# norm_g on the transposed rows: the first token group of a hybrid encoder layer, prepared two chunks at a time

## Chip, core and metric

The kernel runs on one core of one Trainium2 chip. The metric is device time in microseconds (us) of one execution. TensorE is called PE here, VectorE DVE, ScalarE ACT, GpSimd POOL, SyncE SP.

## What is computed

One encoder layer over two inputs, 1024 and 512 tokens of 1024 channels, in fp32. Cut to what matters here:

```python
h = rmsnorm(x, norm_g[l])          # x * rsqrt(mean(x*x) + EPS) * g
p = h @ w_in[l]                    # 1024 -> 4096 columns for three token mixers
y_a = conv_branch(...)             # glu(a_val, a_glu) -> depthwise conv of width 31 -> ...
y_b = sgu_branch(...)
y_c = hgrn_branch(...)
x = x + jnp.concatenate([y_a, y_b, y_c], axis=-1) @ w_out[l]
return rmsnorm(x, final_norm_g)
```

## The kernel before

Tokens stand in three groups of 512, each in four chunks of 128 rows. A matrix product in fp32 precision is made of three products in the fast format fp32r: both operands are split into a high part (a copy rounded to fp32r) and a low part (what the copy lost), and high x high, high x low and low x high are summed. `project` (L195) makes one 128-column tile of `h @ w_in` for one group, or for a half of it (`part`, 256 tokens), with 8 steps of three matmuls, L205 (weights high, tokens high), L206 (weights high, tokens low) and L207 (weights low, tokens high).

`prep` (L283) makes the tokens ready, and this is what the change rewrites for group 0. For each chunk `(g, c)`:

- `squares` (L289): ACT squares the 1024 channels of each row and sums them into `st`.
- `scaled` (L299): POOL makes the reciprocal root in two small operations (`rstd`, L118 and L119); DVE multiplies the rows by it and by `gb`, norm_g broadcast to all 128 partitions (L303). For odd chunks of groups 1 and 2, POOL multiplies by `gb` (`gained`, L295), and DVE by the root alone (L301).
- `turned` (L306): PE transposes the chunk in 8 blocks into two PSUM banks (L313); for each bank ACT writes the high part `hh` (128x512, L316) and DVE the low part `hl` (L317). Once a chunk is turned, `ready[g]` allows products.

`w_split` (L182) splits one weight tile `wr` into `wh` (ACT, L123) and `wl` (POOL, L124) in two halves and issues further weight loads. `warm` (L213) issues matmuls whose result is not used.

The order on ACT, DVE and POOL is the program's order (`manual_schedule`, L440); PE and SP are ordered by the scheduler when the program is built. Tasks such as `prep` are generators: `project` calls `step` every second of its 8 steps when it makes a half group, and `step` resumes a task whose time has come. Before the first product, `prep` prepares chunks 0 and 1 of group 0 and the squares and scaling of chunks 2 and 3; then the transposes of chunks 2 and 3; then, every `PACE` steps, one chunk of groups 1 and 2 (`rest`). The products of the two first column tiles (`pglu`, `pval`) are made for each half of each group.

SP issues the loads in the order x chunk 0, 1, `gb`, two halves of the first weight tile, x chunks 2, 3, the second weight tile, and the chunks of group 1 (L419 to L428).

Of the kernel before, what the change touches and what calls it, by code (L numbers as in the profile page):

```python
# [11 lines left out]
F32 = mybir.dt.float32  # L12
F32R = mybir.dt.float32r
# [7 lines left out]
P = 128  # L21
# [8 lines left out]
PJ = 3  # L30
NGAP = 2
PACE = 3
WARM = (18, 2, 0)
LOW = 32

FIRST = (2, 8, 32)
# [18 lines left out]
def trunk_kernel(ctx, tc, x_prompt, x_sample, norm_g, w_in, conv_w, conv_b, conv_ln_g, conv_ln_b,  # L55
# [25 lines left out]
    def tp_t(name):  # L81
        return ps_tp.tile([P, GRP], F32, tag="tp", name=name)

    def sc_t(name):
        return ps_sc.tile([P, NCH, P], F32, tag="sc", name=name)
# [32 lines left out]
            pool_e.tensor_scalar(out=out, in0=in_, scalar1=mul, scalar2=EPS, op0=ALU.mult, op1=ALU.add)  # L118
        pool_e.tensor_tensor(out=out, in0=out, in1=mexp[:, :n], op=ALU.pow)  # L119

    def split(hi, lo, src):

        act(hi, src, AF.Copy)  # L123
        pool_e.tensor_tensor(out=lo, in0=src, in1=hi.bitcast(F32), op=ALU.subtract)  # L124


# [52 lines left out]
                nc.sync.dma_start(raw, w_src[:, (n % 2) * 4:(n % 2) * 4 + 4, m * P:(m + 1) * P])  # L179
            w_raw.append(raw)  # L180

    def w_split():  # L182
        n = len(w_ready)
        if n < len(tile_order):
            hi = wp.tile([P, KT, P], F32R, tag="hi", name=f"wh{n}")
            lo = wp.tile([P, KT, P], F32R, tag="lo", name=f"wl{n}")
            for a in range(2):
                split(hi[:, 4 * a:4 * a + 4, :], lo[:, 4 * a:4 * a + 4, :], w_raw[2 * n + a])
                w_load()
            w_ready.append((hi, lo))  # L190

    hts = [None] * NG
    ready = [0] * NG

    def project(m, g, name, done, pj=None, part=slice(0, GRP)):  # L195

        hi, lo = w_ready[tile_order.index(m)]
        wait_for(lambda: ready[g] * P >= part.stop)
        his, los = hts[g]
        if pj is None:  # L200
            pj = pj_t(name)
        short = part.stop - part.start < GRP
        for k in range(KT):
            hh, hl = his[k // 4][:, k % 4, part], los[k // 4][:, k % 4, part]
            nc.tensor.matmul(pj[:, part], hi[:, k, :], hh, start=k == 0, stop=False)  # L205
            nc.tensor.matmul(pj[:, part], hi[:, k, :], hl, start=False, stop=False)  # L206
            nc.tensor.matmul(pj[:, part], lo[:, k, :], hh, start=False, stop=k == KT - 1)  # L207
            if k == KT - 1 and part.stop == GRP:
                done(pj)
            if not short or k % 2 == 1:  # L210
                step()

    def warm(n):  # L213

        t = uo_t("warm").rearrange("p c n -> p (c n)")
        for _ in range(n):
            nc.tensor.matmul(t[:, :P], ident, ident, start=True, stop=True)
# [62 lines left out]
        nc.sync.dma_start(xt, xsrc[g][c * P:(c + 1) * P, :])  # L280
        return xt

    def prep(xs, junk_t, gb):  # L283
# [21 lines left out]
        def turned(g, c):  # L305
# [11 lines left out]
                dve.tensor_tensor(out=lo, in0=tp3, in1=hi.bitcast(F32), op=ALU.subtract)  # L317
            ready[g] = c + 1

        warm(WARM[0])  # L320
        squares(0, 0)
        scaled(0, 0)
        squares(0, 1)
        scaled(0, 1)
        w_split()
        turned(0, 0)
        warm(WARM[1])
        turned(0, 1)
        warm(WARM[2])
        squares(0, 2)  # L330
        scaled(0, 2)
        squares(0, 3)
        scaled(0, 3)
        w_split()
        yield 4
        turned(0, 2)
        yield 2
        turned(0, 3)
        yield 1
        rest = [(g, c) for g in range(1, NG) for c in range(NCH)]  # L340
        for i in range(len(rest) + 2):
# [41 lines left out]
    def local_main(l1, accs):  # L383
# [11 lines left out]
        def glu_pair(i, g, parts=(slice(0, GRP),)):  # L395
            sg = sg_t(f"sglu{i}{g}")

            def val_done(pj):
                si, j = where(g)
                dve.tensor_tensor(out=glus[i][si][:, PAD + j * GRP:PAD + (j + 1) * GRP], in0=pj, in1=sg, op=ALU.mult)  # L400

            pg, pv = pj_t(f"pglu{i}{g}"), pj_t(f"pval{i}{g}")
            for part in parts:
                last = g == NG - 1 and part.stop == GRP
                project(A_GLU + i, g, "", lambda pj: act(sg, pj, AF.Sigmoid), pg, part)
                if last:
                    w_split()
                project(A_VAL + i, g, "", val_done, pv, part)
                if last:
                    w_split()  # L410

        with tc.tile_pool(name="xp", bufs=1) as xp:
            def x_t(shape, name):
                return xp.tile(shape, F32, tag="x", name=name, bufs=9)
# [4 lines left out]
            xs = [[] for _ in range(NG)]  # L419
            xs[0].append(load_x(0, 0, x_t))  # L420
            xs[0].append(load_x(0, 1, x_t))
            nc.sync.dma_start(gb, norm_g.broadcast_to((P, DM)))
            w_load()
            w_load()
            for c in range(2, NCH):
                xs[0].append(load_x(0, c, x_t))
            w_load(x_t([P, KT, P], "wr2"))
            xs[1] = [load_x(1, c, x_t) for c in range(NCH)]  # L428
            rows = xp.tile([N_ROWS, P], F32, tag="rows", name="rows")
            for r0, src in ((R_NG, norm_g[0]), (R_CB, conv_b[0]), (R_CLG, conv_ln_g[0]), (R_CLB, conv_ln_b[0]),  # L430
# [8 lines left out]
                    pool_e.memset(glus[i][si][:, PAD + len(gs) * GRP:], 0.0)  # L439
            with tc.manual_schedule(engines={mybir.EngineType.Activation, mybir.EngineType.DVE,  # L440
                                             mybir.EngineType.Pool}):
                task = prep(xs, junk_t, gb)
# [734 lines left out]
```

## Time and profile before

| what | value |
|---|---|
| device time, median of 3 runs | 850.74 us (849.82 to 851.8) |
| device time of the profiled execution | 850.33 us |
| its span, first to last instruction | 848.2 us |
| busy, share of the span: PE / DVE / ACT / POOL | 97% / 58% / 41% / 33% |
| mean granted clock of PE | 0.992 |

The span is 2.1 us shorter than the time of its execution. PE is busy nearly always, but the busy time of an engine is an average over stages; in the first 45 us several engines take turns in setting the pace. The mean granted clock is a share of 2.4 GHz.

### The profile page before, as it was taken

The page shows a single profiled execution, that of the slowest core. Times are in us where ns is not written, and L with a number is a line of the kernel's source. Part 1 is how long each engine was busy: PE and PEld are TensorE (multiplying, and loading weights), DVE is VectorE, ACT ScalarE, POOL GpSimd, SP SyncE. Part 2 cuts the span into 40 slices and gives each one's busy share as a digit, 9 for nine tenths or more (in the row PEclk, how much of TensorE's full clock was granted, in tenths as well). Part 3 has the DMA queues.
Part 4 walks back from the last instruction along what each step waited for, and adds up shares of the span by engine and source line. Part 5 has one row for each costly group of instructions (what it writes and reads, how often), then busy time and mean ns, then how long its engine had stood idle before and what let it go on. Part 6 is the DMA issues. An engine that isn't in the chain of part 4 may idle for free.

```text
span 848.2 us, 17598 instructions
## 1 busy us (share of the span) xinstructions
PE 821.6 (97%) x7249; PEld 704.0 (83%) x7249; DVE 488.5 (58%) x1024; ACT 349.2 (41%) x707; POOL 277.6 (33%) x288
## 2 busy tenths in 40 slices
PE   6999969999999999999999999999999999999996
PEld 6998869877888889998877888899888787888886
DVE  4737767686423378742279855886324888443332
ACT  5725456654334454432244533545123454222221
POOL 5737867999523321031112104211112010111111
PEclk9999979999999999999999999999999999999999
DMA  8305534441112100021010102001111484334421
GB/s 273 139 11 159 160 113 135 138 138 50 49 36 64 51 27 27 3 63 50 16 36 27 39 1 75 27 3 27 40 48 51 200 290 147 123 135 145 145 99 50
DMA packets 63842, 72.35 MB, mean 85 GB/s; under 512 B 3643, under 2 KB 46994, under 8 KB 62738
## 3 DMA queue, kind: packets, MB, share of 16 engines
q1 hardware_dynamic: 63762, 71.23, 25.5%
q8 instruction: 57, 0.93, 0.5%
q14 instruction: 23, 0.19, 0.1%
HBM read 50.25 MB, written 20.97 MB: 84 GB/s over the span
## 4 chain that ended last, share of the span: by engine, by line
PE 81%; DVE 6%; DMA 4%; issue 3%; ACT 3%; POOL 3%; SPq 1%; POOLq 0%; ACTq 0%; DVEq 0%
PE po L1061 5%; PE po L1063 5%; PE po L1062 5%; PE pf L205 5%; PE pf L207 5%; PE pf L206 5%; PE o L975 3%; PE pg L205 2%; DMA wor<-in_w_out_dram 2%; PE pq L205 2%; PE sc L808 2%; PE pg L206 2%; PE pg L207 2%; DVE Q L783 2%; PE pq L206 2%
## 5 line engine op out<-in xcount | busy, mean ns | idle before, releaser
L124 POOL TENSOR_TENSOR wl<-wr,wh 128x512 fp32r<-128x512 f32 x64 | 85.1, 1341 | 161.1 <-ACT wh L123 156.3
L476 DVE SCALAR_TENSOR_TENSOR ca<-glu,par,ca 128x512 f32<-128x512 f32 x120 | 80.6, 747 | 0.0
L1061 PE MATMUL po<-woh,yh 128*128 128x512 f32 (+1 forms) x200 | 77.4, 387 | 0.0
L205 PE MATMUL pf<-hh,wh 128*128 128x512 f32 x192 | 76.8, 400 | 0.0
L1062 PE MATMUL po<-wol,yh 128*128 128x512 f32 (+1 forms) x200 | 76.2, 381 | 0.0
L1063 PE MATMUL po<-woh,yl 128*128 128x512 f32 (+1 forms) x200 | 76.1, 381 | 0.0
L207 PE MATMUL pf<-hh,wl 128*128 128x512 f32 x192 | 75.0, 391 | 0.0
L206 PE MATMUL pf<-hl,wh 128*128 128x512 f32 x192 | 74.8, 390 | 0.0
L789 ACT ACTIVATE kc<-K 128x512 f32<-128x512 f32 x84 | 56.3, 674 | 40.3 <-DVE K L783 36.7
L501 POOL TENSOR_TENSOR part<-part,pr 128x512 f32<-128x512 f32 x54 | 68.5, 1285 | 3.8 <-ACT pr L500 3.8
L783 DVE TENSOR_TENSOR Q<-Q,T 128x256 f32<-128x256 f32 x144 | 65.4, 495 | 2.9 <-ACT q L819 2.0
L123 ACT ACTIVATE wh<-wr 128x512 fp32r<-128x512 f32 x64 | 39.0, 627 | 50.8 <-PE pf L206 20.6
L783 DVE TENSOR_TENSOR K<-K,T 128x256 f32<-128x256 f32 x144 | 54.9, 422 | 5.8
L727 DVE TENSOR_SCALAR Q<-Q,oml,lbt 128x512 f32<-128x512 f32 x24 | 17.8, 742 | 64.7 <-ACT Q L724 64.7
L1067 DVE TENSOR_TENSOR yx<-po,yx 128x512 f32<-128x512 f32 (+1 forms) x25 | 16.7, 669 | 56.1 <-PE po L1063 56.1
L780 POOL TENSOR_TENSOR ks<-K 128x512 f32<-128x512 f32 x12 | 16.4, 1365 | 99.6 <-ACT kc L789 53.7
L1063 PEld LDWEIGHTS po<-woh,yl 128*128 128x128 f32 x200 | 37.6, 188 | 7.5 <-DVE yl L1042 0.2
L1062 PEld LDWEIGHTS po<-wol,yh 128*128 128x128 f32 x200 | 37.7, 188 | 6.9
L1061 PEld LDWEIGHTS po<-woh,yh 128*128 128x128 f32 x200 | 37.6, 188 | 6.8
L207 PEld LDWEIGHTS pf<-hh,wl 128*128 128x128 f32 x192 | 36.0, 188 | 7.8
L1079 POOL TENSOR_TENSOR stf<-stf 128x1 f32<-128x1 f32 x12 | 4.1, 340 | 117.2 <-ACT yx L1068 117.2
L205 PEld LDWEIGHTS pf<-hh,wh 128*128 128x128 f32 x192 | 36.1, 188 | 7.0
(366 smaller groups left out, 2278.2 us busy)
## 6 DMA issues: line engine op xcount, KB each, us to landing
wr<-in_w_in_dram SPq DMA_DIRECT2D x62, 256.0 KB
out_dram<-yx SPq DMA_DIRECT2D x24, 256.0 KB
yx<-yd SPq DMA_DIRECT2D x12, 448.0 KB
x<-in_x_prompt_dram SPq DMA_DIRECT2D x8, 512.0 KB
wor<-in_w_out_dram SPq DMA_DIRECT2D x16, 256.0 KB
wod<-woh SPq DMA_DIRECT2D x16, 256.0 KB
wod<-wol SPq DMA_DIRECT2D x16, 256.0 KB
woh<-wod SPq DMA_DIRECT2D x4, 1024.0 KB
```

The costliest lines, as they stand in the source:

```text
L123: act(hi, src, AF.Copy)
L124: pool_e.tensor_tensor(out=lo, in0=src, in1=hi.bitcast(F32), op=ALU.subtract)
L205: nc.tensor.matmul(pj[:, part], hi[:, k, :], hh, start=k == 0, stop=False)
L206: nc.tensor.matmul(pj[:, part], hi[:, k, :], hl, start=False, stop=False)
L207: nc.tensor.matmul(pj[:, part], lo[:, k, :], hh, start=False, stop=k == KT - 1)
L476: dve.scalar_tensor_tensor(out=acc, in0=src, scalar=col(R_CW + 2 * t + i), in1=acc, op0=ALU.mult, op1=ALU.add)
L501: pool_e.tensor_tensor(out=parts[g], in0=parts[g], in1=pr, op=ALU.add)
L783: dve.tensor_tensor(out=x, in0=x, in1=y, op=ALU.mult)
L789: act(view(kc, 0, [[2 * m, n2], [m, 2], [1, m]]), view(K, 0, [[2 * m, n2], [GRP + m, 2], [1, m]]), AF.Copy)
L1061: nc.tensor.matmul(po, yh[:, k, :], hi[:, ns], start=k == 0, stop=False)
L1062: nc.tensor.matmul(po, yh[:, k, :], lo[:, ns], start=False, stop=False)
L1063: nc.tensor.matmul(po, yl[:, k, :], hi[:, ns], start=False, stop=k == KT - 1)
```

## The change

For group 0 alone, the rows are multiplied by the reciprocal root only (`scaled_first`, L353). norm_g is loaded as 8 rows of 128, issued from ACT's own queue, turned by PE into `gcol`, one column per block of 128 channels, and applied while the transposed rows leave PSUM: ACT writes the high part with `scale=gcol[:, k]`, DVE the low part as `src * gcol[:, k] - hi` (`gained_first`, L335). This is done for two chunks (256 tokens) at a time, and so per block of channels: a PSUM bank holds two blocks of 256 tokens. The broadcast `gb` is still loaded for groups 1 and 2, now behind the loads of group 0. The second weight tile is loaded before x chunks 2 and 3, and split inside `gained_first` with DVE in ACT's place. The first `pglu` and `pval` of group 0 put their eight matmuls with low weights last. The warm-up matmuls are 6 and 8 in place of 18 and 2.

```diff
-WARM = (18, 2, 0)
+WARM = (6, 8)
...
-    def split(hi, lo, src):
+    def split(hi, lo, src, by_vector=False):
 
-        act(hi, src, AF.Copy)
+        if by_vector:
+            dve.tensor_copy(hi, src)
+        else:
+            act(hi, src, AF.Copy)
         pool_e.tensor_tensor(out=lo, in0=src, in1=hi.bitcast(F32), op=ALU.subtract)
...
-            nc.tensor.matmul(pj[:, part], lo[:, k, :], hh, start=False, stop=k == KT - 1)
+            if not low_last:
+                nc.tensor.matmul(pj[:, part], lo[:, k, :], hh, start=False, stop=k == KT - 1)
+            elif k == KT - 1:
+                for j in range(KT):
+                    nc.tensor.matmul(pj[:, part], lo[:, j, :], his[j // 4][:, j % 4, part],
+                                     start=False, stop=j == KT - 1)
...
+        def turned_first(c0, tiles):
+            for c in (c0, c0 + 1):
+                for k in range(KT):
+                    o = (k % 2) * 256 + (c - c0) * P
+                    nc.tensor.transpose(tiles[k // 2][:, o:o + P], xs[0][c][:, k * P:(k + 1) * P], ident)
+                yield 1
+
+        def gained_first(c0, tiles, between=None):
+            his, los = hts[0]
+            ts = slice(c0 * P, (c0 + 2) * P)
+            for k in range(KT):
+                src = tiles[k // 2][:, (k % 2) * 256:(k % 2 + 1) * 256]
+                hi, lo = his[k // 4][:, k % 4, ts], los[k // 4][:, k % 4, ts]
+                act(hi, src, AF.Copy, scale=gcol[:, k:k + 1])
+                dve.scalar_tensor_tensor(out=lo, in0=src, scalar=gcol[:, k:k + 1], in1=hi.bitcast(F32),
+                                         op0=ALU.mult, op1=ALU.subtract)
+                if k == 5 and between:
+                    between()
+            ready[0] = c0 + 2
...
         warm(WARM[0])
-        squares(0, 0)
-        scaled(0, 0)
-        squares(0, 1)
-        scaled(0, 1)
+        gp = uo_t("gp").rearrange("p c n -> p (c n)")
+        nc.tensor.transpose(gp[:, :KT], gr, ident[:KT, :KT])
+        dve.tensor_copy(gcol, gp[:, :KT])
+        warm(WARM[1])
+        hts[0] = [[big.tile([P, 4, GRP], F32R, tag="H", name=f"h{e}0{a}") for a in range(2)] for e in "hl"]
+        for c in range(2):
+            squares(0, c)
+            scaled_first(c)
         w_split()
-        turned(0, 0)
...
-        turned(0, 1)
...
-        squares(0, 2)
-        scaled(0, 2)
-        squares(0, 3)
-        scaled(0, 3)
-        w_split()
-        yield 4
-        turned(0, 2)
-        yield 2
-        turned(0, 3)
+        tiles = four("txa")
+        for _ in turned_first(0, tiles):
+            pass
+        gained_first(0, tiles, lambda: w_split(True))
+        for c in range(2, NCH):
+            squares(0, c)
+            scaled_first(c)
+        yield 6
+        tiles = four("txb")
+        yield from turned_first(2, tiles)
+        gained_first(2, tiles)
         yield 1
...
-            nc.sync.dma_start(gb, norm_g.broadcast_to((P, DM)))
+            gr = xp.tile([KT, P], F32, tag="gr", name="gr")
+            gcol = xp.tile([P, KT], F32, tag="gcol", name="gcol")
+            nc.scalar.dma_start(gr, norm_g[0].rearrange("(r j) -> r j", j=P))
             w_load()
             w_load()
+            w_load(x_t([P, KT, P], "wr2"))
             for c in range(2, NCH):
                 xs[0].append(load_x(0, c, x_t))
-            w_load(x_t([P, KT, P], "wr2"))
+            nc.sync.dma_start(gb, norm_g.broadcast_to((P, DM)))
```

`yield 6` is the value that the first `next(task)` returns; it isn't used, as `yield 4` wasn't.

How the change moves instructions, at three places. First ACT, from the high parts of group 0's first half to the squares of group 1's first chunk. `hh` is the high part of the tokens, `tx`, `txa` and `txb` are PSUM tiles with transposed rows, `jx,st` the squares. Before:

```order
6 L316 ACTIVATE hh_194<-tx_198 128x4x128 [waits PE_49]
7 L316 ACTIVATE hh_195<-tx_205 128x4x128 [waits PE_49]
8 L316 ACTIVATE hh_194<-tx_215 128x4x128 [waits PE_49]
9 L316 ACTIVATE hh_195<-tx_222 128x4x128 [waits PE_49]
10 L289 ACTIVATE jx_231,st_230<-x_119 128x1024 [waits DMAHW5_49,Activation_49]
11 L289 ACTIVATE jx_237,st_236<-x_121 128x1024 [waits DMAHW6_49,Activation_49]
```

Now, for the second half of group 0 (the first half has the same eight rows with `txa`):

```order
17 L342 ACTIVATE hh_175<-txb_274,gcol 128x256 [waits PE_49]
18 L342 ACTIVATE hh_175<-txb_274,gcol 128x256 [waits DVE_49]
19 L342 ACTIVATE hh_175<-txb_275,gcol 128x256 [waits PE_49]
20 L342 ACTIVATE hh_175<-txb_275,gcol 128x256 [waits DVE_49]
21 L342 ACTIVATE hh_176<-txb_276,gcol 128x256 [waits PE_49]
22 L342 ACTIVATE hh_176<-txb_276,gcol 128x256 [waits DVE_49]
23 L342 ACTIVATE hh_176<-txb_277,gcol 128x256 [waits PE_49]
24 L342 ACTIVATE hh_176<-txb_277,gcol 128x256 [waits DVE_49]
25 L297 ACTIVATE jx_331,st_330<-x_128 128x1024 [waits DMAHW1_49,Activation_49,Pool_49]
```

Four operations of 128x512 per half have become eight of 128x256, and the second in each bank has got a wait for DVE: for the DVE operation that reads the bank's first block. DVE in turn waits for ACT before each of its own.

Second POOL, around the second weight tile (`wl_234`, before `wl_243`) and the roots `st` of chunks 2 and 3. Before:

```order
23 L118 TENSOR_SCALAR st_230<-st_230 128x1 [waits Activation_49]
24 L119 TENSOR_TENSOR st_230<-st_230,mexp 128x1 [waits Pool_49]
25 L118 TENSOR_SCALAR st_236<-st_236 128x1 [waits Activation_49]
26 L119 TENSOR_TENSOR st_236<-st_236,mexp 128x1 [waits Pool_49]
27 L124 TENSOR_TENSOR wl_243<-wr_123,wh_242 128x512 [waits DMAHW7_49,Activation_49]
28 L124 TENSOR_TENSOR wl_243<-wr_123,wh_242 128x512 [waits Activation_49]
```

Now:

```order
23 L127 TENSOR_TENSOR wl_234<-wr_121,wh_233 128x512 [waits DMAHW5_49,DVE_49]
24 L127 TENSOR_TENSOR wl_234<-wr_121,wh_233 128x512 [waits DVE_49]
25 L118 TENSOR_SCALAR st_247<-st_247 128x1 [waits Activation_49]
26 L119 TENSOR_TENSOR st_247<-st_247,mexp 128x1 [waits Pool_49]
27 L118 TENSOR_SCALAR st_253<-st_253 128x1 [waits Activation_49]
28 L119 TENSOR_TENSOR st_253<-st_253,mexp 128x1 [waits Pool_49]
```

The two subtractions for the weights stood behind the roots of chunks 2 and 3 and now stand ahead of them; they wait for DVE's copies, which stand on DVE between the sixth and the seventh low part of the first half.

Third PE, where group 0 ends and group 1 begins; `tx_386` and `tx_393` hold chunk 0 of group 1, `tx_426` and `tx_433` chunk 1, `tx_465` and `tx_472` chunk 2. Now:

```order
103 L209 MATMUL pval_269<-hl_178,wh_233 128x256
104 L211 MATMUL pval_269<-hh_176,wl_234 128x256
105 L321 MATMUL tx_386<-ident,x_128 128x128 x4
106 L321 MATMUL tx_393<-ident,x_128 128x128 x4
107 L321 MATMUL tx_426<-ident,x_130 128x128 x4
108 L321 MATMUL tx_433<-ident,x_130 128x128 x4
109 L208 MATMUL pglu_480<-hh_382,wh_191 128x256
110 L321 MATMUL tx_465<-ident,x_132 128x128 x4
111 L321 MATMUL tx_472<-ident,x_132 128x128 x4
```

All products of group 0 now stand ahead of the transposes of group 1. Before, chunk 0's transposes stood 36 products ahead of the end of group 0 and chunk 1's 18. Behind the squares of group 1's chunk 0, the orders on ACT, DVE, POOL and SP are what they were, to the end of the program, and so is PE's from the transposes of group 1's chunk 3 on.

## Rows read from the trace of the kernel before

**Rows 1.** The page's first part, busy time of PE and its neighbours.
```profile
PE 821.6 (97%) x7249; PEld 704.0 (83%) x7249; DVE 488.5 (58%) x1024; ACT 349.2 (41%) x707; POOL 277.6 (33%) x288
```
**Rows 2.** Chain that ended last, 0 to 130 us: start, duration, what.
```profile
30.09 3.41 POOL x L295
...
36.39 2.94 DVE x L303
...
60.20 2.55 POOL wl L124 x2
```
**Rows 3.** Timeline of PE, 0 to 62 us: start, duration, what, idle before and releaser.
```profile
25.34 1.04 PE L313 MATMUL tx<-ident,x 128*128 128x128 f32 x8
29.00 1.06 PE L313 MATMUL tx<-ident,x 128*128 128x128 f32 x8 [0.47 <-DVE x L301]
...
39.47 1.06 PE L313 MATMUL tx<-ident,x 128*128 128x128 f32 x8 [0.91 <-DVE x L303]
```
**Rows 4.** Timeline of ACT, 0 to 60 us.
```profile
4.37 1.06 ACT L289 ACTIVATE jx<-x 128x1024 bf16<-128x1024 f32 x1 [2.37 <-DMA x<-in_x_prompt_dram]
...
5.67 1.06 ACT L289 ACTIVATE jx<-x 128x1024 bf16<-128x1024 f32 x1
...
10.90 0.64 ACT L123 ACTIVATE wh<-wr 128x512 fp32r<-128x512 f32 x1 [0.87 <-DMA wr<-in_w_in_dram]
11.44 2.04 ACT L316 ACTIVATE hh<-tx 128x512 fp32r<-128x512 f32 x4
...
21.53 1.06 ACT L289 ACTIVATE jx<-x 128x1024 bf16<-128x1024 f32 x1
```
**Rows 5.** Timeline of DVE, 0 to 60 us.
```profile
12.05 2.48 DVE L317 TENSOR_TENSOR hl<-tx,hh 128x512 fp32r<-128x512 f32 x4 [1.75 <-ACT hh L316]
...
23.62 1.28 DVE L303 SCALAR_TENSOR_TENSOR x<-x,st,gb 128x1024 f32<-128x1024 f32 x1 [1.14 <-POOL st L119]
...
28.10 0.75 DVE L301 TENSOR_SCALAR x<-x,st 128x1024 f32<-128x1024 f32 x1 [3.20 <-POOL st L119]
```
**Rows 6.** Timeline of POOL, 0 to 60 us.
```profile
17.40 3.48 POOL L124 TENSOR_TENSOR wl<-wr,wh 128x512 fp32r<-128x512 f32 x2
...
27.24 0.19 POOL L118 TENSOR_SCALAR st<-st 128x1 f32<-128x1 f32 x1
27.51 0.55 POOL L119 TENSOR_TENSOR st<-st,mexp 128x1 f32<-128x1 f32 x1
28.15 0.75 POOL L118 TENSOR_SCALAR st<-st 128x1 f32<-128x1 f32 x1
```
**Rows 7.** Groups of equal shape, whole span: count, busy us, mean ns of one, idle before.
```profile
L123 ACT ACTIVATE wh<-wr 128x512 fp32r<-128x512 f32 x64 | 39.0, 627 | 50.8 <-PE pf L206 20.6 <-issue 17.5 <-DMA wr<-in_w_in_dram 10.3
...
L497 ACT ACTIVATE part<-glu,par 128x512 f32<-128x512 f32 x6 | 4.2, 712 | 2.2 <-DVE par L450 2.2
...
L752 ACT ACTIVATE V<-pi01b 128x256 f32<-128x256 f32 x1 | 0.4, 385 | 0.1
```
**Rows 8.** The same view: ACT with two operands per partition, and DVE's forms.
```profile
L379 ACT ACTIVATE xn<-ta,rsa 128x256 f32<-128x256 f32 x12 | 6.2, 561 | 15.6 <-DVE rsa L374 8.9 <-issue 6.8
...
L476 DVE SCALAR_TENSOR_TENSOR ca<-glu,par,ca 128x512 f32<-128x512 f32 x120 | 80.6, 747 | 0.0
...
L729 DVE TENSOR_SCALAR K<-K,oml 128x512 f32<-128x512 f32 x24 | 19.6, 818 | 0.0
...
L917 DVE SCALAR_TENSOR_TENSOR S<-S,tot,U 128x128 f32<-128x128 f32 x48 | 16.7, 348 | 8.6 <-PE U L908 7.0
...
L829 DVE TENSOR_TENSOR Q<-q,T 128x256 f32<-128x256 f32 x12 | 5.0, 420 | 0.0
```
**Rows 9.** Stretches: length, busy of PE, PEld, DVE, ACT, POOL, granted clock, DMA.
```profile
50.00:60.00 10.00, 10.00 (x85) 10.00 (x84) 1.73 (x3) 1.29 (x3) 0.00 (x0) 1.00 0.01 2
...
110.00:120.00 10.00, 3.92 (x18) 3.92 (x19) 2.31 (x9) 5.52 (x9) 6.40 (x7) 0.56 0.40 116
120.00:130.00 10.00, 10.00 (x80) 10.00 (x79) 9.26 (x16) 4.93 (x9) 6.98 (x6) 0.93 0.24 80
```

More of the change, by code (lines that the diff above doesn't have):

```diff
@@ L180, in w_load, with w_split @@
             w_raw.append(raw)
-    def w_split():
+    def w_split(by_vector=False):
         n = len(w_ready)
@@ L187, in w_split @@
             for a in range(2):
-                split(hi[:, 4 * a:4 * a + 4, :], lo[:, 4 * a:4 * a + 4, :], w_raw[2 * n + a])
+                split(hi[:, 4 * a:4 * a + 4, :], lo[:, 4 * a:4 * a + 4, :], w_raw[2 * n + a], by_vector)
                 w_load()
@@ L193, in trunk_kernel, with project @@
     ready = [0] * NG
-    def project(m, g, name, done, pj=None, part=slice(0, GRP)):
+    def project(m, g, name, done, pj=None, part=slice(0, GRP), low_last=False):
         hi, lo = w_ready[tile_order.index(m)]
@@ L281, in load_x, with prep @@
         return xt
-    def prep(xs, junk_t, gb):
+    def prep(xs, junk_t, gb, gr, gcol):
         sts = {}
@@ L318, in turned @@
             ready[g] = c + 1
-        warm(WARM[0])
-        squares(0, 0)
-        scaled(0, 0)
-        squares(0, 1)
-        scaled(0, 1)
-        w_split()
-        turned(0, 0)
-        warm(WARM[1])
-        turned(0, 1)
-        warm(WARM[2])
-        squares(0, 2)
-        scaled(0, 2)
-        squares(0, 3)
-        scaled(0, 3)
-        w_split()
-        yield 4
-        turned(0, 2)
-        yield 2
-        turned(0, 3)
+        def turned_first(c0, tiles):
[4 more added lines that the diff above has]
+                yield 1
@@ new lines, in four, with scaled_first @@
+        def four(name):
+            return [tp_t(f"{name}{j}") if j % 2 == 0 else sc_t(f"{name}{j}").rearrange("p c n -> p (c n)")
+                    for j in range(4)]
+        def scaled_first(c):
+            st = sts[0, c]
+            rstd(st, st, 1, 1.0 / DM)
+            dve.tensor_scalar(out=xs[0][c], in0=xs[0][c], scalar1=st, scalar2=None, op0=ALU.mult)
+        warm(WARM[0])
+        gp = uo_t("gp").rearrange("p c n -> p (c n)")
+        nc.tensor.transpose(gp[:, :KT], gr, ident[:KT, :KT])
@@ L404, in glu_pair @@
                 last = g == NG - 1 and part.stop == GRP
-                project(A_GLU + i, g, "", lambda pj: act(sg, pj, AF.Sigmoid), pg, part)
+                first = i == 0 and g == 0 and part.start == 0
+                project(A_GLU + i, g, "", lambda pj: act(sg, pj, AF.Sigmoid), pg, part, first)
                 if last:
                     w_split()
-                project(A_VAL + i, g, "", val_done, pv, part)
+                project(A_VAL + i, g, "", val_done, pv, part, first)
                 if last:
@@ L441, in local_main @@
                                              mybir.EngineType.Pool}):
-                task = prep(xs, junk_t, gb)
+                task = prep(xs, junk_t, gb, gr, gcol)
                 next(task)
```

## The prediction

> **What bounds the kernel.** I read the page first, then the chain of waits, then the timelines of the engines in the first 60 us. The page's first part shows PE busy for 97% of the span [rows 1], so a change of the first 20 us lasts only if it moves PE's later work. The chain of the work that ended last says who moves it: from 30 to 39 us it isn't PE but the preparation of groups 1 and 2, POOL's multiplication by gb and DVE's scaling of a group 2 chunk [rows 2]. PE's timeline says the same: it waits 0.47 us for chunk 1 of group 1 and 0.91 us for chunk 0 of group 2 (transposes at 39.47) [rows 3]. Later PE has no gap for long (50 to 60 us: 10.00 of 10 [rows 9]), and at 60.20 POOL starts on the next weights when PE leaves the old ones [rows 2]. The orders of all engines behind these transposes are unchanged, so I take a shift there to reach the end whole.
>
> The reader should therefore look at when the preparation of group 1 begins: ACT's squares of its chunk 0, at 21.53 [rows 4]. Chunk 0 of group 2 is transposed 17.9 us later, and in between stands a chain of ACT, POOL and DVE which the change does not touch. **The question is where 21.53 goes.**
>
> **The change part by part.** *Loads.* gb (512 KB) leaves the queue ahead of the weights; a load of that size takes 1.30 us (squares of chunks 0 and 1 begin at 4.37 and 5.67, when each lands) [rows 4]. So the second half of the first weight tile, which ACT awaited until 10.90, lands at 9.60, and ACT, which began the next operation 0.54 later [rows 4], begins the high parts at 10.14. Chunks 0 and 1 are scaled and turned by then, since they no longer wait for gb; the small load, the turn of gr and the copy to gcol lie in the first 5 us, when PE runs only warm-up, and cost nothing. If they were late, they would push this 10.14.
>
> *Prices.* No row has ACT on 128x256 of PSUM with one scale per partition. Without it a 128x256 took 0.385; a scale costs 0.712 less 0.627, 0.085, on 128x512 [rows 7]. I take 0.47; the ends are 0.385 and the 0.561 of the form with two such operands [rows 8]. DVE's three-operand form with one input in PSUM took 0.348 for 128 columns and 0.747 for 512 [rows 8]; between them 256 take 0.48, with 0.42 of the two-operand form [rows 8] as low end. Four of ACT's 128x512 took 2.04 and four of DVE's 2.48 [rows 4, 5], and these rows' own lengths (0.60, 0.68) mean that starts overlap by 0.12 and 0.08. A handover costs 0.04 (POOL ends at 28.06, DVE starts at 28.10) [rows 5, 6].
>
> The Trainium skill (ScalarE: Activation LUTs, What ACT_TABLE_LOAD costs) gives 186 ns plus 0.833 ns per column, and 93 ns for a per-partition operand, so 0.49 as an estimate from that page. By it the sum would be 0.2 us higher.
>
> *One half of group 0.* Before, four ACT operations, 0.48 apart. Now the two blocks of a bank alternate strictly, ACT, DVE, ACT, DVE, by the waits in the order. The first two blocks: 0.47 + 0.04 + 0.48 + 0.04 = 1.03 between ACT's starts. From one bank to the next: ACT's second block 0.47, handover 0.04, DVE's second and third block 0.40 apart (0.48 less 0.08), then 0.48 and handover 0.04, together 1.43. ACT's next work starts 1.03 + 3 x 1.43 + 0.35 = **5.67 us** after a half began, where before a half took 1.9.
>
> The Trainium skill (PSUM — Partial Sum Buffer, PSUM bank collisions raise a hardware error) forbids two engines in one bank at a time, reads included. By that rule the waits cannot be dropped while two blocks share a bank, and it speaks against the layout; no row here has such a pair.
>
> *Second weight tile.* DVE makes two 128x512 copies after its sixth block. That form isn't in the trace; a 128x1024 TENSOR_SCALAR took 0.75 [rows 5] and a 128x512 one 0.818 [rows 8]. I take 0.50, nearer to the first, which also goes from SBUF to SBUF (ends 0.38 and 0.82). They delay the last bank by 2 x 0.42 = 0.84. ACT is freed of its two splits, which is counted in its order. The sixth block starts on ACT at 10.14 + 1.03 + 2 x 1.43 = 14.03, on DVE at 14.54, the copies at 14.94, and they end at 15.86. POOL's two subtractions, before behind the roots of chunks 2 and 3, now stand ahead of them: 2.55 [rows 2] (high end 3.48 [rows 6]) to 18.45. The squares of chunk 2 start at 10.14 + 5.67 + 0.84 = 16.65 and are no longer late then.
>
> *Chunks 2 and 3.* A root takes 0.19 + 0.08 + 0.55 = 0.82 [rows 6], with handover to 19.35; DVE scales chunk 2 until 20.1 (0.75). POOL's next small operation is held while DVE does that, as at 28.15, where it took 0.75 in place of 0.19 [rows 6]; the root of chunk 3 is ready at 20.75, the chunk at 21.55. PE turns it from 21.7, ACT starts the second half 0.4 later (two of the chunk's eight blocks, 1.05 in all, and a handover), at **22.1**, and the squares of group 1 start at 22.1 + 5.67 = **27.8**.
>
> *Products with low weights last, warm-up.* No work is added but the turn of gr: the same 48 matmuls, only ordered, and fewer warm-ups. They change what PE does while it waits; I cost them at nothing, since PE waits for the preparation in any case. If that cover were gone, the low products' order would cost nothing still.
>
> **Sum.** 27.8 less 21.53 is 6.3 us late. Back come 0.3: chunk 0 of group 1 was ready at 24.90 [rows 5] but turned only at 25.34 [rows 3], since products stood ahead; with 0.14 of handover (39.33 to 39.47 [rows 2, 3]) it could have been 25.04, and now nothing stands ahead. That leaves **+6.0 us** on the profiled execution's 850.33, **856.3 us** (the median, 850.74, is 0.41 above that execution). Waits of PE grow by as much, less what its products no longer cover.
>
> With all low ends (gb worth 2.6, twice a load, and POOL not held) the same steps give the half 4.8, the squares at 24.1 and 852.5. With all high ends (gb worth 0, since the load's place may not be what made the weights late) they give a half of 6.1, 31.5 and 860.0.
>
> **Rivals.** *PE sets the pace, faster.* If the preparation were early enough, PE's work alone would count. For it: high parts begin at 10.1, not 11.44 [rows 4], and 36 products that stood between the transposes of group 1 are done earlier. PE would end group 0 at 28.5, then 36 products at 0.118 (85 in 10 us [rows 9]) and five turned chunks at 1.05 [rows 3] lead to 38.0, against 39.47 + 1.06 = 40.53: 2.5 us less, **847.8**. This needs the squares of group 1 at 19.2 or earlier; at 21.8 nothing is won or lost. Against it: POOL's order alone puts the second half of group 0 behind 18.45. It would need ACT and DVE not to alternate, and the copies early. Chance 0.07.
>
> *Nothing measurable.* Low prices throughout, and one more saving: DVE's scaling at 36.39 took 2.94 beside POOL [rows 2], while the same form took 1.28 [rows 5]; if the new timing parts them, 1.66 come back. Together with the low ends, 852.5 becomes 850.8. Chance 0.06.
>
> *The clock falls as well.* PE is idle in the new order from 28.5 to 31.3 and again for some 3 us before chunk 1 of group 1. Before, after a long wait (PE busy 3.92 of 10 us) the granted clock averaged 0.56 over 110 to 120 us and 0.93 over 120 to 130 [rows 9], so PE was at its 1.2 GHz level for some 5 us, and products took twice as long there: 18 in 3.92 us, 0.22 each, against 0.118. Were that to happen at 39 to 45 us, some 25 products would lose 0.1 each: +2.5, **858.8**. Against it: each idle stretch here is half of the 6.1 us that PE lacks in that row, and transposes stand between them. Chance 0.13.
>
> The Trainium skill (TensorE: Matmul & The Clock Gate, Part 1: The HAM clock gate) says that an idle array falls to half its clock; by that rule this rival holds, and the stretch at 110 us agrees.
>
> **Numbers.** Forecast 856.3 with chance 0.74. The range, 852.8 to 860.2, is what the ends of the prices span, cut a little where all would have to fall on one side, and it takes in the clock's case; it leaves out the faster one. A measurement can tell about 0.2% (1.7 us). Slower: 0.74 + 0.13 = 0.87; same 0.06; faster 0.07.
>
> **What would show it.** In the new profile: ACT's high parts from about 10.1, alternating with DVE at 1.43 per bank; POOL's weights ending near 18.4 and the root of chunk 3 after 20; squares of group 1 near 27.8; PE idle for 2 to 3 us twice between 28 and 36, and the transposes of group 2's chunk 0 near 45.5; from there the old spacing. I am wrong if group 1's squares start before 22, if PE does not wait for these chunks, or if the idle stretch in 110 to 120 us [rows 9] shrinks by as much as the start is late.

## The result and the profile after

| | kernel before | changed kernel |
|---|---|---|
| device time, median | 851.27 us (849.82 to 852.5) | 858.89 us (857.98 to 859.2) |
| profiled execution / its span | 850.33 / 848.2 us | 859.2 / 857.0 us |
| mean granted clock of PE | 0.992 | 0.986 |

The changed kernel is slower: the ratio is 1.0088, with a 95% interval of 1.0069 to 1.0108. The forecast was 856.3 us with a range of 852.8 to 860.2. The medians differ by 7.6 us; the two profiled executions, from which the rows come, by 8.87.

The page's first part hardly moves [rows 1]; PE's and DVE's busy time grow by 6.3 and 2.7 us, and nothing in it says where.

```profile
PE 827.9 (97%) x7238; PEld 708.3 (83%) x7238; DVE 491.2 (57%) x1035; ACT 351.7 (41%) x713; POOL 276.0 (32%) x288
```

ACT's timeline of the changed kernel does (start, duration, what, idle before and releaser; the rows that answer to rows 4).

```profile
10.95 0.47 ACT L342 ACTIVATE hh<-txa,gcol 128x256 fp32r<-128x256 f32 x1 [2.21 <-PE txa L333]
11.98 0.84 ACT L342 ACTIVATE hh<-txa,gcol 128x256 fp32r<-128x256 f32 x2 [0.55 <-DVE hl L343]
13.39 0.84 ACT L342 ACTIVATE hh<-txa,gcol 128x256 fp32r<-128x256 f32 x2 [0.58 <-DVE hl L343]
...
17.27 1.05 ACT L297 ACTIVATE jx<-x 128x1024 bf16<-128x1024 f32 x1
...
22.59 0.47 ACT L342 ACTIVATE hh<-txb,gcol 128x256 fp32r<-128x256 f32 x1 [3.14 <-PE txb L333]
...
28.25 1.05 ACT L297 ACTIVATE jx<-x 128x1024 bf16<-128x1024 f32 x1
```

The reader should see three things. ACT idles 0.55 to 0.58 us for DVE before every second block: one bank per 1.41 to 1.42 us (11.98 to 13.39). The undisturbed half lasts from 22.59 to 28.25, 5.66 us. And group 1's squares start at 28.25, 6.72 later than the 21.53 of rows 4.

POOL's timeline of the changed kernel shows what stands ahead of the roots of chunks 2 and 3, and two of its multiplications further on.

```profile
7.89 2.95 POOL L127 TENSOR_TENSOR wl<-wr,wh 128x512 fp32r<-128x512 f32 x2
16.22 2.67 POOL L127 TENSOR_TENSOR wl<-wr,wh 128x512 fp32r<-128x512 f32 x2 [5.38 <-DVE wh L124]
18.97 0.19 POOL L118 TENSOR_SCALAR st<-st 128x1 f32<-128x1 f32 x1
...
19.88 0.75 POOL L118 TENSOR_SCALAR st<-st 128x1 f32<-128x1 f32 x1
...
30.50 3.32 POOL L303 TENSOR_TENSOR x<-x,gb 128x1024 f32<-128x1024 f32 x1 [0.21 <-ACT jx L297]
...
36.54 2.36 POOL L303 TENSOR_TENSOR x<-x,gb 128x1024 f32<-128x1024 f32 x1 [0.35 <-ACT jx L297]
```

And DVE's timeline of the changed kernel, where two of these meet a scaling:

```profile
7.96 1.75 DVE L356 TENSOR_SCALAR x<-x,st 128x1024 f32<-128x1024 f32 x1 [0.72 <-POOL st L119]
...
15.72 0.75 DVE L124 CAST wh<-wr 128x512 fp32r<-128x512 f32 x2
...
21.30 0.75 DVE L356 TENSOR_SCALAR x<-x,st 128x1024 f32<-128x1024 f32 x1 [0.72 <-POOL st L119]
...
30.33 1.28 DVE L311 SCALAR_TENSOR_TENSOR x<-x,st,gb 128x1024 f32<-128x1024 f32 x1 [1.47 <-POOL st L119]
...
36.62 3.35 DVE L311 SCALAR_TENSOR_TENSOR x<-x,st,gb 128x1024 f32<-128x1024 f32 x1
```

PE's timeline of the changed kernel answers to rows 3:

```profile
8.72 2.85 PE L333 MATMUL txa<-ident,x 128*128 128x128 f32 x16
...
31.77 1.07 PE L321 MATMUL tx<-ident,x 128*128 128x128 f32 x8 [1.69 <-DVE x L311]
...
35.65 1.94 PE L321 MATMUL tx<-ident,x 128*128 128x128 f32 x8 [2.82 <-DVE x L309]
...
40.12 1.94 PE L321 MATMUL tx<-ident,x 128*128 128x128 f32 x8 [2.12 <-DVE x L311]
...
45.16 1.03 PE L321 MATMUL tx<-ident,x 128*128 128x128 f32 x8
...
48.19 1.04 PE L321 MATMUL tx<-ident,x 128*128 128x128 f32 x8
```

The last row is chunk 0 of group 2: 48.19 instead of 39.47, 8.72 later, and the span is 8.8 longer. So the loss was complete at 48 us and reached the end whole. It splits at the rows above: 6.43 stood at chunk 0 of group 1 (31.77 against 25.34); 0.22 came by chunk 1 (35.65), 1.41 by chunk 2 (40.12) and 1.76 by chunk 3 (45.16); then 1.10 came back, since chunk 0 of group 2 no longer waits. The stretches (columns as in rows 9) show the clock between 30 and 50 us:

```profile
30.00:40.00 10.00, 3.50 (x18) 2.71 (x17) 6.53 (x6) 7.70 (x14) 9.04 (x8) 0.73 0.02 7
40.00:50.00 10.00, 9.88 (x67) 9.91 (x68) 7.41 (x11) 5.53 (x11) 6.62 (x9) 0.76 0.01 2
```

PE was busy for 3.50 of the first 10 us. The granted clock was 0.50, its 1.2 GHz level, from 34.6 to 44.8 us, and 1.00 behind that; at the lower level 8 transposes took 1.94 us instead of 1.04.

### The profile page after: what moved, and what is told of

Read it like the earlier page. It is cut to its first block, busy times and chain, and to the rows that moved or that the text cites. A ratio compares the mean times of both kernels' runs of the same rounds, so it can differ in the third digit from the quotient of the medians.

```text
span 857.0 us, 17596 instructions
## 1 busy us (share of the span) xinstructions
PE 827.9 (97%) x7238; PEld 708.3 (83%) x7238; DVE 491.2 (57%) x1035; ACT 351.7 (41%) x713; POOL 276.0 (32%) x288
## 4 chain that ended last, share of the span: by engine, by line
PE 79%; DVE 6%; DMA 3%; issue 3%; ACT 2%; POOL 2%; SPq 0%; POOLq 0%; ACTq 0%; DVEq 0%
PE po L1105 5%; PE po L1107 5%; PE po L1106 5%; PE pf L208 5%; PE pf L211 5%; PE pf L209 5%; PE o L1019 3%; PE pg L208 2%; DVE Q L827 2%; PE sc L852 2%; PE pq L208 2%; PE pg L209 2%; PE pg L211 2%; PE U L952 2%; PE pq L209 2%
```

## The experiments

The theory: group 1's squares are late for two reasons, the alternation inside a bank and POOL's order, and that sets the time. The rivals: the order of the products, the order of the loads, PE's clock. Each kernel is the changed one with the edit shown, unless said otherwise; ratios are to the kernel before.

**Blocks in different banks.**

```diff
-                    o = (k % 2) * 256 + (c - c0) * P
-                    nc.tensor.transpose(tiles[k // 2][:, o:o + P], xs[0][c][:, k * P:(k + 1) * P], ident)
+                    o = (k // 4) * 256 + (c - c0) * P
+                    nc.tensor.transpose(tiles[k % 4][:, o:o + P], xs[0][c][:, k * P:(k + 1) * P], ident)
...
-                src = tiles[k // 2][:, (k % 2) * 256:(k % 2 + 1) * 256]
+                src = tiles[k % 4][:, (k // 4) * 256:(k // 4 + 1) * 256]
```

> Consecutive blocks of two channel partitions' columns lie in different PSUM banks; nothing else is changed. Theory (group 1's first squares, at 28.25 us in the changed kernel, set the time, and the alternation of ACT and DVE within a bank is the largest part of their delay): ACT's blocks come every 0.5 to 0.6 us instead of two per 1.42 us, the first half's last one ends near 15 instead of 17.27, the second half takes about 3.9 instead of 5.7, the squares start at 24.5 to 25.5, and the time falls by 2.8 to 4.0 us, to about 855.4. Rival 1 (POOL's weight subtractions ahead of the roots of chunks 2 and 3 set it): the first half gets shorter, chunk 3 is scaled as late as before (22.06), the squares start at 26.5 to 27.0 and 1.2 to 1.8 us are gained. Rival 2 (the squares do not matter, the product order or the throttled clock of TensorE does): 858.9 within 0.6.

Measured: 853.85 us, ratio 1.0039 (1.0024 to 1.0054), clear of the changed kernel's interval. ACT's timeline of this run:

```profile
10.58 3.02 ACT L342 ACTIVATE hh<-txa,gcol 128x256 fp32r<-128x256 f32 x8 [1.45 <-PE txa L333]
13.45 1.10 ACT L297 ACTIVATE jx<-x 128x1024 bf16<-128x1024 f32 x1
...
20.61 3.03 ACT L342 ACTIVATE hh<-txb,gcol 128x256 fp32r<-128x256 f32 x8 [4.93 <-PE txb L333]
23.47 1.11 ACT L297 ACTIVATE jx<-x 128x1024 bf16<-128x1024 f32 x1
```

Eight high parts follow each other without a wait, and ACT's next work starts 2.86 us after a half began, where 5.66 were needed. The squares start at 23.47, 4.78 earlier. Of these, 0.37 is an earlier first high part (10.58 against 10.95); counted from the first high part, the squares come after 12.89 us instead of 17.30. The medians fall by 5.0 us; by the ratios, each to the kernel before in its own session, it is 4.2 us. Both are more than I had expected (2.8 to 4.0): I had put ACT's blocks 0.5 to 0.6 apart, and they are 0.36 apart. The layout, with blocks that ACT and DVE read in turn in one bank, is the largest part of the loss.

**The second weight tile behind chunks 2 and 3, alone and with the banks.**

```diff
-        gained_first(0, tiles, lambda: w_split(True))
+        gained_first(0, tiles)
         for c in range(2, NCH):
             squares(0, c)
             scaled_first(c)
+        w_split(True)
```

> The second weight tile is split after chunks 2 and 3 are scaled, so that POOL's two subtractions stand behind the two roots and DVE's two copies behind the scaling; nothing else is changed. Theory: ACT's first half is about 0.8 us shorter (no copies of DVE in it), chunk 3 is scaled near 20.6 instead of 22.06, group 1's squares start at 26.8 instead of 28.25, and the time falls by 1.2 to 1.8 us, to about 857.4. Rival 1 (only the alternation within a bank matters, POOL's order is hidden): squares at 27.4 or later, at most 0.8 gained. Rival 2 (TensorE needs the second weight tile earlier than it then comes): TensorE waits for it near 22 us, and the time is the same or longer.

> Both edits together: blocks in different banks, and the second weight tile split after chunks 2 and 3 are scaled. Theory: the two gains nearly add up: first half done near 14.5, chunk 3 scaled near 18.5, second half 19.5 to 23.4, group 1's squares at 23.4 to 24.2 (28.25 in the changed kernel, 21.53 in the kernel before), time 853.8 to 855.0, still some 2.5 to 4 us above the kernel before. Rival (a part of the loss is the throttled clock and the longer waits behind it, not the squares): more than 856.

Measured: alone 857.38 us, ratio 1.0086 (1.0069 to 1.0103), not told apart from the changed kernel; squares at 27.45, 0.80 earlier, which is rival 1's "27.4 or later". Counted from the first high part, 0.95 is gained, and 0.67 of it is that ACT's wait before its last block of the first half, which held DVE's copies, fell from 1.25 to 0.58 us. With different banks 851.20 us, ratio 1.0005 (0.9994 to 1.0015), clear of the banks alone and level with the kernel before. Here the squares start at 22.27, 10.97 us after the first high part, 1.92 less than with the banks alone, and what is left is where PE waits between 15 and 60 us. PE's waits of this run (engine, line, who is waited for: us in all, times, longest):

```profile
PE tx L321 <- DVE x L311: 2.4, 3, 1.3
PE tx L321 <- DVE x L309: 1.6, 1, 1.6
```

In the changed kernel the same two lines hold 3.8 and 2.8 us. So the place of the second weight tile matters once ACT and DVE are quick; the edit moves DVE's copies together with POOL's subtractions, and no run moves them apart. The two edits together undo the change's loss as far as the time can tell: the interval reaches up to 1.3 us, and group 2's chunk 0 is still turned 1.28 later than before (40.75 against 39.47). The largest step on the way, 1.4 us, is at chunk 2, whose scaling still takes 3.37 us beside POOL. The time is 2.6 us below the lower end of what I had expected: each half again took 2.87 us, not the 3.9 of my sum.

**Products with low weights in their old order.**

```diff
-            if not low_last:
+            if True:
```

> Group 0's first products again take the low weights with each partition of channels, not last; nothing else is changed. Theory: nothing, 858.9 within 0.6, group 1's squares at 28.25 within 0.3, since TensorE waits for the first group's halves with either order. Rival (the product order costs or saves time): TensorE waits for the low weights (17.6 and 18.9 us) or runs earlier through its products, and the time moves by more than 1 us.

Measured: 858.59 us, ratio 1.0096 (1.0081 to 1.0112), squares at 27.68. That is outside my 0.3, but the first high part came 0.54 earlier too (10.41); from there to the squares it is 17.27 us against 17.30. The order of the products costs and saves nothing that can be told.

**PE kept busy where it waits.**

```diff
             if i >= 2:
+                warm({(1, 0): 10, (1, 1): 18, (1, 2): 13}.get(rest[i - 2], 0))
                 turned(*rest[i - 2])
```

> The changed kernel with 10, 18 and 13 idle products of the identity put ahead of the transposes of chunks 0, 1 and 2 of group 1, where TensorE waits 1.69, 2.82 and 2.12 us; nothing else is changed. Theory (the later squares of group 1 are most of the loss, the throttled clock after the idle stretch is an add-on): the granted clock stays at 1.00 from 30 to 50 us (0.73 and 0.76 in the changed kernel), the products behind the transposes of chunk 2 take 0.12 us each instead of 0.214, the transposes of group 2's chunk 0 start 1.3 to 2.0 us earlier than 48.19, and the time falls by 1.0 to 2.0 us, to about 857.3. Rival 1 (the clock is no loss of its own, it only falls where TensorE waits anyway): 858.9 within 0.6. Rival 2 (the clock is the loss): 853 or less.

Measured: 858.61 us, ratio 1.0097 (1.0077 to 1.0118). The median is rival 1's; the interval, some 857.0 to 860.4 us, holds the theory's 857.3 as well, so the time alone doesn't decide. The same stretches in this run:

```profile
30.00:40.00 10.00, 7.15 (x63) 6.79 (x62) 6.85 (x7) 6.68 (x12) 9.09 (x9) 1.00 0.01 3
40.00:50.00 10.00, 10.00 (x90) 10.00 (x88) 8.07 (x12) 6.55 (x13) 7.20 (x8) 1.00 0.01 2
```

The clock stays up, though the idle products did not all run where PE waits: PE's order is the scheduler's, and 28 of the 41 ran at 10.9 to 15.5 and 25.3 to 30.2 us (the profile counts two for each). PE still waits 2.36 us for chunk 1, and the last 13 hold chunk 2:

```profile
37.19 3.06 PE L225 MATMUL warm<-ident 128*128 128x128 f32 x26
40.09 1.04 PE L321 MATMUL tx<-ident,x 128*128 128x128 f32 x8
...
43.12 1.04 PE L321 MATMUL tx<-ident,x 128*128 128x128 f32 x8
```

DVE had scaled this chunk by 39.22; turned at 40.09, it is only 0.03 earlier than in the changed kernel, although the squares came 0.80 earlier (27.45). Behind it the lower clock is gone: chunk 3 follows after 3.03 us instead of 5.04, and group 2's chunk 0 is turned at 46.16, 2.03 earlier. So by the trace the clock costs the changed kernel 2.0 us at 45 us. Yet the span is 0.7 shorter only. PE's waits behind 50 us show where a part went: at the gating value's second group it waits for ACT's evictions of the first. The first row is of the changed kernel,

```profile
PE pbv1a L237 <- ACT vn L636: 7.7, 1, 7.7
```

and this one of the run with PE kept busy:

```profile
PE pbv1a L237 <- ACT vn L637: 8.5, 1, 8.5
```

The last experiment returns to this wait.

**The load of norm_g's copies in its old place.**

```diff
+            nc.sync.dma_start(gb, norm_g.broadcast_to((P, DM)))
             w_load()
             w_load()
...
-            nc.sync.dma_start(gb, norm_g.broadcast_to((P, DM)))
             xs[1] = [load_x(1, c, x_t) for c in range(NCH)]
```

> The changed kernel with the load of norm_g's 128 copies back ahead of the weights; nothing else is changed. Theory: the weights land near 9.4 and 10.9 us again instead of 6.6 and 8.1, ACT's weight copies in front of the first high parts end near 11.5, the first high part starts there instead of 10.95, and everything behind it moves by 0.4 to 0.8 us: time 859.2 to 859.9. Rival (the early weights collide with DVE's scaling of chunk 1, which took 1.75 us, and with the lower clock of the 16 transposes, so that they gain nothing): the first high part at 10.9 or earlier, 858.9 within 0.5. The prediction's own figure, 1.30 us for the load's removal, would give 860.2.

Measured: 859.35 us, ratio 1.0108 (1.0091 to 1.0125), not told apart from the changed kernel. ACT's timeline of this run:

```profile
10.02 0.63 ACT L126 ACTIVATE wh<-wr 128x512 fp32r<-128x512 f32 x1 [0.32 <-DMA wr<-in_w_in_dram]
11.06 0.47 ACT L342 ACTIVATE hh<-txa,gcol 128x256 fp32r<-128x256 f32 x1 [0.41 <-PE txa L333]
```

The weights land 1.9 us later than in the changed kernel (10.02 against 8.12) and the first high part starts 0.11 later: it waits for PE's transposes either way. The time lies in both ranges; the start, 11.06, is nearer to the rival's (10.9 or earlier) than to the theory's (11.5), and the prediction's 1.30 us were not there. The other change in the order of loads, the second weight tile ahead of x chunks 2 and 3, was not undone by itself; ACT's squares of chunk 2 follow its last high part without idle time (17.27), so they did not wait for a load.

**No multiplication on POOL: with the two edits above, and in the kernel before.**

```diff
         def by_pool(g, c):
-            return g and c % 2 == 1
+            return False
```

> Blocks in different banks and the second weight tile after chunks 2 and 3 (851.2 us), and besides groups 1 and 2 scale all chunks on DVE, so that POOL multiplies no chunk by norm_g. Theory (once group 1's squares are as early as 22.3 us, what is left between them and group 2 is POOL's 3.3-us multiplications: chunk 1 behind them, chunk 2's DVE scaling of 3.36 us beside one): chunk 2's scaling takes 1.28 again, the transposes of chunks 1 to 3 follow 3.0 to 3.3 us apart, those of group 2's chunk 0 start at 38 to 38.8 instead of 40.75, and the time is 848.3 to 849.5, 0.2 to 0.3% below the kernel before. Rival (DVE becomes the bound with four scalings of 1.28 us a group): the transposes are more than 3.4 us apart and the time is 851 or more.

> The kernel before, in which groups 1 and 2 scale all chunks on DVE as well; no part of the change. Theory (the kernel before loses only the waits of 0.47 and 0.91 us in group 1's and 2's transposes to POOL's multiplications, rows 3): the transposes of group 2's chunk 0 start near 38.3 instead of 39.47 and the time is 849.0 to 850.2. Rival 1 (these multiplications, not the change, are what the two versions at 848 gained): 848.5 or less. Rival 2 (four DVE scalings a group of 1.28 us, where rows 5 show the queue of DVE full behind chunk 3's high parts, hold TensorE): 851.5 or more.

Measured: 847.91 us, ratio 0.9976 (0.9966 to 0.9987), with the change and its two edits; 848.91 us, ratio 0.9976 (0.9968 to 0.9985), without the change. PE's timeline of the first run:

```profile
26.06 1.06 PE L321 MATMUL tx<-ident,x 128*128 128x128 f32 x8 [0.87 <-DVE x L311]
...
28.27 1.04 PE L321 MATMUL tx<-ident,x 128*128 128x128 f32 x8
...
31.30 1.03 PE L321 MATMUL tx<-ident,x 128*128 128x128 f32 x8
...
34.50 1.06 PE L321 MATMUL tx<-ident,x 128*128 128x128 f32 x8
```

Only chunk 0 is waited for, and the others follow 2.2 to 3.2 us apart. Group 2's chunk 0 is turned at 37.55, and at 36.74 in the other run; both this and the times are slightly better than expected. Both kernels end at the same ratio, with gains of 0.29% and 0.24% that the intervals don't tell apart, so this gain belongs to POOL's multiplications and not to the change.

**The change carried through.** Groups 1 and 2 are prepared by pairs of chunks too, with both edits above, so that `gb` is not loaded at all:

```diff
-        rest = [(g, c) for g in range(1, NG) for c in range(NCH)]
+        pairs = [(g, c) for g in range(1, NG) for c in (0, 2)]
...
+                tiles = four(f"tx{g}{c0}")
+                yield from turned_first(c0, tiles, g)
+                gained_first(c0, tiles, None, g)
```

> The change carried through: groups 1 and 2 too turn two chunks at a time and take norm_g from the partition scalars, blocks in different banks, the second weight tile after chunks 2 and 3, no load of the 128 copies, no multiplication on POOL. Theory: group 1's squares near 22.3, its four chunks scaled by 28, its pairs' high parts 3.0 us each, TensorE's waits between 24 and 40 us shrink from some 4 us to 1 to 2, and the time is 846.5 to 849.5, below the kernel before. Rival (ACT's and DVE's eight 256-column parts a pair, 3.0 to 3.2 us, hold TensorE, which needs 6 us of work a pair, or the transposes wait for the banks of the pair before): 851 or more.

Measured: 848.48 us, ratio 0.9979 (0.9970 to 0.9988), as expected; PE's waits in 15 to 60 us are

```profile
PE pglu L209 <- DVE hl L343: 1.2, 1, 1.2
PE txb L333 <- DVE x L356: 1.2, 2, 1.0
```

It is no faster than the version that leaves groups 1 and 2 by chunks and spares POOL.

**The start.** Two edits, in the last two versions:

```diff
-WARM = (6, 8)
+WARM = (4, 4)
...
-        for c in range(2):
-            squares(0, c)
-            scaled_first(c)
+        squares(0, 0)
+        scaled_first(0)
+        squares(0, 1)
+        st = sts[0, 1]
+        rstd(st, st, 1, 1.0 / DM)
+        act(xs[0][1], xs[0][1], AF.Copy, scale=st)
```

> The change carried through to all groups (848.48 us), and at the start chunk 1 is scaled by ACT instead of DVE, and 8 warming products stand where 14 did. Theory (the first high part came at 10.95, not 10.14, because DVE's scaling of chunk 1 took 1.75 us beside POOL's subtraction, and because the warming products held the 16 transposes until 8.72): chunk 1 is scaled by 9.1 instead of 9.71, chunk 0 is turned from 7.4, the first high part comes at 10.1 to 10.4, everything behind it moves by 0.6 to 0.9, and half of that or more reaches the time: 847.6 to 848.2. Rival (fewer warming products leave the clock low, and the transposes take longer): the first high part at 10.9 or later, 848.5 or more.

> The version without POOL's multiplications (847.91 us) with the same two edits at the start. Theory: first high part at 10.1 to 10.4 instead of 11.3, time 847.0 to 847.6. Rival as in the run beside it: 847.9 or more.

Measured: 848.85 us, ratio 0.9974 (0.9963 to 0.9985), with the pairs, a miss for the theory; 847.43 us, ratio 0.9958 (0.9944 to 0.9971), without them, as expected in the time, though the interval still touches that of the version without these edits, and that of the kernel before without POOL's multiplications. So whether the mended change is worth anything by itself stays open; if so, it is some 0.2%. PE's timeline of the first of the two:

```profile
7.31 3.84 PE L333 MATMUL txa<-ident,x 128*128 128x128 f32 x16 [0.94 <-DVE x L356]
```

The transposes start 1.41 earlier than in the changed kernel, but take 3.84 us instead of 2.85, so the high parts come at 10.55, and at 10.44 in the other. So both halves of the expectation hold: warming products held the transposes, and with fewer of them the transposes are slower.

**The wait behind.** From the fastest version, w_out's halves are loaded one ahead:

```diff
+            def load(n):
+                raw = lp.tile([P, GRP], F32, tag="wor", name=f"wor{n // 2}{n % 2}", bufs=2)
...
+            raws = [load(0)]
...
-                    raw = lp.tile([P, GRP], F32, tag="wor", name=f"wor{k}{a}")
-                    nc.sync.dma_start(raw, w_out[0, k * P:(k + 1) * P, ns])
                     yield 4
+                    raw = raws.pop()
+                    if 2 * k + a < 2 * KT - 1:
+                        raws.append(load(2 * k + a + 1))
```

> The fastest version so far (847.43 us), in which w_out's halves are also loaded one half ahead into two buffers instead of one. Theory (what TensorE gained ahead of 60 us came only partly to the end, because it waits at the second group of the gating value, 8.9 us, for ACT's evictions of the first group, and these stand in ACT's queue behind a high part of w_out whose load, issued after the half before it was written, lands every 6.3 us): ACT's waits for these loads between 60 and 125 us fall from 18.7 us to less than 6, the evictions come at 106 to 109 instead of 114, TensorE's wait falls to 2 to 5 us, and the time to 842 to 845. Rival (ACT's queue is held by POOL's partial sums and the taps of DVE as well, or the loads only get slower side by side): the evictions at 112 or later, 846.5 or more.

The chain that ended last in the changed kernel names what was suspected (start, duration, what):

```profile
118.21 3.82 DMA wor<-in_w_out_dram
122.14 0.63 ACT woh L126
122.77 0.61 ACT pr L544
123.40 1.28 ACT L636
124.69 0.39 ACT vn L636
125.13 0.58 PE pbv1a L237
```

Measured: 843.40 us, ratio 0.9909 (0.9895 to 0.9922), the fastest of all kernels here. Waits of the version it starts from,

```profile
ACT woh L126 <- DMA wor<-in_w_out_dram: 18.7, 4, 7.0
...
PE pbv1a L237 <- ACT vn L640: 8.9, 1, 8.9
```

and of this one:

```profile
ACT woh L126 <- DMA wod<-woh: 7.9, 3, 5.6
...
PE pbv1a L237 <- ACT vn L647: 4.4, 1, 4.4
```

The load is gone from ACT's longest waits (a write-back takes its place), the evictions come at 108.71 instead of 113.96, PE waits 4.5 us less, and 4.0 us come to the end. So this chain of w_out's loads, ACT and POOL holds PE a second time. In the program it starts behind group 2's products of the first two column tiles, so it moves with a late start as a whole (w_out's first high part at 76.85 in the changed kernel, 68.36 before); a gain that comes to PE alone is partly waited away there. That it swallowed a part of the clock's 2.0 us is argued from the wait, 8.5 us against 7.7, and was not tried by itself; neither was this edit on the kernel before.

## Why the prediction was right, and where its sizes were off

- *The mechanism.* The question was where 21.53 goes; the answer, 27.8, was measured as 28.25. Undoing the alternation moved the squares by 4.78 us (4.41 from the first high part) and the time by 4.2 to 5.0; moving the second weight tile's copies and subtractions back besides brought the time to the kernel before's, within 1.3 us. So these two are shown to be what made the squares late, and most of the loss. The clock's loss goes with them (1.00 from 30 to 50 us in that run); the collision below stays.
- *The half.* Forecast 5.67, measured 5.66, and its terms too: 1.03 for the first bank, 1.42 for the others. DVE's operation took 0.48, as forecast from its neighbours. DVE's copies were put at 2 x 0.42, and took 0.75 together. POOL's subtractions were to end at 18.45 and ended at 18.89; the small operation behind was held for 0.75, as in rows 6.
- *gb's removal, 1.30.* Mis-sized. The weights came 2.8 us earlier (ACT's copy at 8.12 against 10.90), but the high parts began at 10.95 and not at 10.14: "chunks 0 and 1 are scaled and turned by then" failed. DVE scaled chunk 1 in 1.75 us beside POOL's subtraction, and PE began its 16 transposes only at 8.72, behind the warming products. With the load in its old place the start was 11.06, so the load was worth 0.1. That a start 0.81 late became squares only 0.45 late is partly luck: the copies were shorter than forecast, and POOL's first subtraction began when one copy was done (16.22), not both.
- *The 0.3 that come back.* They did: from squares to chunk 0's transposes 3.52 us, before 3.81.
- *"A chain which the change does not touch."* Its order was untouched, its durations were not: chunk 2 came 1.41 later still. Its scaling, 1.28 in rows 5, met POOL's next multiplication and took 3.35. The prediction had such a collision in the kernel before's row of 2.94 [rows 2], and counted only on its going away. This is the term that was missing. What decided was 0.2 us: before, DVE had started at 29.97 and POOL at 30.09; now POOL was first.
- *The clock.* The rival's place was right (14 of the 17 products behind chunk 2 were 0.21 us apart, forecast 25), and so was its size in the trace: 2.0 us at chunk 3, forecast 2.5. The argument against it, that each idle stretch is only half of the 6.1 us in its row, did not hold: the clock fell at 34.6, in PE's wait of 2.82 us for chunk 1. Its 858.8 is nearer to the measured 858.89 than the forecast's 856.3, but that nearness is luck, since the collision and the waits that vanish are in neither. How much of the 2.0 us reaches the end stays open: the run that kept the clock up is not told apart from the changed kernel. In the row of its price [rows 9], 0.56 and 0.93 make some 10 us at the lower level, not 5; PE worked in about half of them.
- *The sum.* Forecast +6.0 on the profiled execution, measured +8.87: 0.4 from the squares, 0.2 at chunk 1, 1.4 from the collision, and the rest is the slow clock less the waits that vanish (1.76 and 1.10 at chunks 3 and 0). The medians, 7.6 apart, lie nearer to the forecast than this pair of executions. *PE sets the pace, faster* needed squares at 19.2; the fastest version has 21.51, and is faster for other reasons.
- *The rule on banks.* The Trainium skill (PSUM — Partial Sum Buffer, PSUM bank collisions raise a hardware error) was weighed as speaking against this layout. No run here breaks the rule, so none shows what would happen; that a half takes 2.86 us with consecutive blocks in different banks, instead of 5.66, shows what waiting in turn inside a bank costs.

## What to carry to other kernels

When two engines read the same PSUM tile one after the other, lay consecutive pieces into different banks: the work was the same, and each half became 2.8 us shorter. When work moves to another engine, look at what it releases: POOL's subtractions came forward with DVE's copies and stood before two roots that others waited for. And look for the next place that PE waits at before costing a gain: of 2.0 us won ahead of 50 us, 0.7 were left in the span.

## What the runs showed of the hardware

- DVE and POOL hold each other up. POOL's multiplication of a chunk took 2.36 us when it started 0.08 before DVE's scaling, which then took 3.35 and ended 1.07 behind it. When DVE started 0.17 ahead, DVE took 1.28 and POOL 3.32. So the "3.4-us" operation of rows 2 is one of 2.4 and a wait. The Trainium skill (SBUF — State Buffer, Who interferes with whom) says that DVE and GpSimd share a pair of ports under an exclusive lock, that a DVE instruction with two inputs in SBUF contends with a GpSimd one that reads SBUF, and that the order of issue decides who blocks; the trace agrees, 3.35 us for DVE when it was second and 1.28 when it was first.
- The recorded clock misses the start. It reads 1.00 for the first 10 us in both the changed kernel and the run with banks apart, while the second lot of 8 warming products (x16 in the profile) took 3.78 us in the one and 2.11 in the other:

```profile
5.15 3.78 PE L225 MATMUL warm<-ident 128*128 128x128 f32 x16 [0.26 <-DVE gcol L361]
```

This row is of the changed kernel, and this one of the run with banks apart:

```profile
5.15 2.11 PE L225 MATMUL warm<-ident 128*128 128x128 f32 x16 [0.26 <-DVE gcol L361]
```

So what looks like the same start differs by up to 1 us from run to run: first high parts at 10.18 to 11.10 in the four kernels that share the changed kernel's loads and layout up to there, and at 10.58 to 11.54 in four with the banks apart. That is why the squares are counted from the first high part above.
